# A sum of squared differences: other rows to other partitions, and the semaphores cleared by another engine

## The chip, the core and the metric

The kernel runs on one core of a Trainium2 chip. The metric is the device time of one execution in microseconds (us). The engines that matter are DVE (VectorE: subtracts), ACT (ScalarE: squares and sums), SP (SyncE: issues the transfers), POOL (GpSimd: sets four constants at the start) and the core's 16 DMA engines.

## The reference

```python
batch, dim = 1024, 4096
x, y: float32 of [batch, dim]
def reference(x, y, axis):        # axis = -1
    return np.sum((x - y) ** 2, axis=axis).astype(np.float32)
```

Two matrices of 16.8 MB each are read, and 1024 sums of 4 KB in all are written.

## The kernel before

**Layout.** There are 1024 rows for 128 partitions, so R = 8 rows lie together in one block of R x D = 32768 floats, 128 KiB, and each partition works on one block. The views `xv`, `yv` and `ov` (lines 60 to 62) say which: partition p takes block p. In SBUF the tensors X and Y hold six of the eight rows of a partition (`H = 6 * D`); the last two rows go into the places of the first two, when those are done with (`home`).

**Loads.** All 15 loads are issued by SP on one queue, each a column range of all 128 partitions (`load`, line 107). X comes in 6 ranges and Y in 9, with widths written out by hand: the first ones are 16384 and 16224 columns (64 KB and 63 KB per partition), then 8192, and then ever smaller ones down to 160 columns, so that little work is left after the last one. The first two are issued ahead of the program's opening barrier (`early`). The loads of the last two rows wait on L215 until ACT has squared the first and the second row.

**Work.** DVE waits for a range of Y and the X that goes with it, and subtracts in place, one row or part of a row at a time (`sub`, L170). ACT squares and sums each of these pieces (`square`, L176). Rows 6 and 7 come in several pieces; their partial sums lie in `parts` and are added by DVE (`complete`, L183). The last piece, of 160 columns, DVE squares and sums itself (L199).

**The end.** SP waits until the sums are there, issues the store of `results` (L227), and then calls `close` (lines 40 to 45):

```python
engine.sem_clear(range(self.sems[0].num, self.sems[-1].num + 1))
engine.wait_ge(stored, value).then_inc(stored, -value)
```

The first line sets the kernel's semaphores back to zero, as the next execution needs them. The semaphore `stored`, which the store counts up, isn't among them; the wait itself takes its 16 off again. There is no barrier at the end; the program is over when each engine has done its last instruction.

## Time and profile before

| | us |
|---|---|
| median of 3 runs (lowest to highest) | 84.36 (84.32 to 84.52) |
| the profiled execution | 84.36 |
| its span, from the first to the last instruction | 83.0 |
| DVE busy | 36.3 |
| ACT busy | 31.7 |
| POOL busy | 0.2 |
| DMA engines in use, as a share of 16 over the span | 95.2% |
| first subtraction on DVE | 40.89 |
| store issued on SP | 81.58 |

The span is shorter than the time, because the runtime opens and closes the program around it. A packet is what one DMA engine moves in one go; its record has a start, a duration and a size. "L170" is line 170 of the kernel.

### The profile page before, as it was taken

What the parts mean: (1) busy time and instruction counts of PE and PEld (TensorE: products, weight loads), DVE (VectorE), ACT (ScalarE), POOL (GpSimd) and SP (SyncE); (2) the same over time, 40 slices, a digit from 0 to 9 for tenths busy, and PEclk for the clock granted to TensorE, in tenths of its full rate; (3) what the DMA queues carried; (4) which work ended last, traced back from release to release, by engine and by line L of the source; (5) the groups of instructions that cost most, each with busy time, mean ns of one, the idle gap of its engine ahead of it and who ended that gap; (6) DMA issues with size and microseconds to landing.
All of it is one profiled execution on the core that took longest, in us unless ns stands there. A gap on an engine that the chain in (4) does not pass through costs nothing.

```text
span 83.0 us, 109 instructions
## 1 busy us (share of the span) xinstructions
DVE 36.3 (44%) x18; ACT 31.7 (38%) x27; POOL 0.2 (0%) x4
## 2 busy tenths in 40 slices
DVE  0000000000000000000299999999099995979981
ACT  0500000000000000000001969798970796989991
POOL 0000000000000000000000000000000000000000
DMA  9299999929999997599799979979999999999940
GB/s 505 95 410 505 505 505 505 505 95 410 500 500 500 500 500 313 219 469 500 332 426 505 474 316 474 505 332 426 424 429 429 400 435 439 426 407 404 395 145 2
DMA packets 2304, 33.56 MB, mean 404 GB/s; under 512 B 384, under 2 KB 768, under 8 KB 1408
## 3 DMA queue, kind: packets, MB, share of 16 engines
q1 hardware_dynamic: 2304, 33.56, 95.2%
HBM read 33.55 MB, written 0.00 MB: 404 GB/s over the span
## 4 chain that ended last, share of the span: by engine, by line
DMA 68%; ACT 14%; DVE 14%; SPq 1%; issue 0%
DMA Y<-in_y_dram 68%; ACT X L176 14%; DVE X L170 14%; SPq L107 1%; DVE results L183 0%; SPq L215 0%
## 5 line engine op out<-in xcount | busy, mean ns | idle before, releaser
L170 DVE TENSOR_TENSOR X<-X,Y 128x4096 f32<-128x4096 f32 (+9 forms) x14 | 35.8, 2593 | 44.9 <-DMA Y<-in_y_dram 44.8
L176 ACT ACTIVATE X<-X 128x4096 f32<-128x4096 f32 (+8 forms) x13 | 29.7, 2288 | 47.7 <-DVE X L170 47.7
L176 ACT ACTIVATION_READ_ACCUMULATOR X<-X 128x1 f32 x13 | 2.4, 188 | 0.0
L176 ACT ACT_TABLE_LOAD x1 | 1.3, 1283 | 1.9 <-PEq L19 1.9
L183 DVE TENSOR_REDUCE results<-parts 128x1 f32<-128x2 f32 (+1 forms) x2 | 0.3, 154 | 0.2 <-ACT X L176 0.2
L199 DVE CUSTOM_DVE_ANT_0 Y<-X,parts 128x160 f32<-128x160 f32 x1 | 0.4, 385 | 0.0
L245 POOL MEMSET const-bfloat16-1.0<- 128x1 bf16 x1 | 0.1, 102 | 0.0
L245 POOL MEMSET const-uint8-127<- 128x1 uint8 x1 | 0.1, 102 | 0.0
L245 POOL MEMSET const-float32-0.0<- 128x1 f32 x1 | 0.1, 99 | 0.2 <-issue 0.2
L245 POOL MEMSET const-float32-1.0<- 128x1 f32 x1 | 0.1, 99 | 0.0
L199 DVE DVE_READ_ACCUMULATOR2_ANT results<- 128x1 f32 x1 | 0.1, 83 | 0.0
## 6 DMA issues: line engine op xcount, KB each, us to landing
Y<-in_y_dram SPq DMA_DIRECT2D x1, 8112.0 KB, 40.4
X<-in_x_dram SPq DMA_DIRECT2D x1, 4096.0 KB, 48.7
Y<-in_y_dram SPq DMA_DIRECT2D x1, 4096.0 KB, 58.0
X<-in_x_dram SPq DMA_DIRECT2D x1, 2784.0 KB, 13.4
Y<-in_y_dram SPq DMA_DIRECT2D x1, 1456.0 KB, 19.2
Y<-in_y_dram SPq DMA_DIRECT2D x1, 1328.0 KB, 16.2
X<-in_x_dram SPq DMA_DIRECT2D x1, 912.0 KB, 21.0
Y<-in_y_dram SPq DMA_DIRECT2D x1, 464.0 KB, 21.6
```

The source lines that it names most:

```text
L107: nc.sync.dma_start(out=dst[:, home(c0, c1)], in_=src[:, c0:c1]).then_inc(sem, 16)
L170: nc.vector.tensor_sub(out=a, in0=a, in1=Y[:, home(c0, c1)]).then_inc(diffs, 1)
L176: nc.scalar.activation(out=a, in_=a, func=Square, accum_out=acc).then_inc(acts, 1)
L183: nc.vector.tensor_reduce(out=results[:, r : r + 1], in_=parts_of(r, len(row_parts[r])), axis=mybir.AxisListType.X, op=add,).then_inc(sums, 1)
L199: nc.vector.tensor_tensor_reduce(out=Y[:, home(*piece)], in0=X[:, home(*piece)], in1=X[:, home(*piece)], scale=1.0, scalar=parts_of(r, 1), ...
L245: nc = _bacc.Bacc("TRN2", target_bir_lowering=False, num_devices=1)
```

## The change

It has two parts, and some code is written in another way without another effect (`pieces_of` is written out where it was called, and `complete(6)` stands without its loop).

The first part is the layout. Partition p = 8e + i takes block 16i + e of the rows in place of block p, with e from 0 to 15 and i from 0 to 7. The source of a load is therefore an array of three dimensions, [16, 8, columns], whose first step is one block (128 KiB) and whose second is 16 blocks (2 MiB), while the destination stays [128, columns]. The store's destination is viewed in the same way.

The second part is the end. POOL waits for the store and then clears the semaphores, with `stored` now among them; SP's clear and SP's wait are gone.

```diff
-    def close(self, engine, stored, value):
-        engine.sem_clear(range(self.sems[0].num, self.sems[-1].num + 1))
-        engine.wait_ge(stored, value).then_inc(stored, -value)
+    def close(self, sem, value):
+        self.nc.gpsimd.wait_ge(sem, value)
+        self.nc.clear_and_free_semaphores(self.sems)
...
-    xv = x.rearrange("(p r) d -> p (r d)", p=P)
-    yv = y.rearrange("(p r) d -> p (r d)", p=P)
-    ov = out.rearrange("(p r) -> p r", p=P)
+    G = 8
+    xv = x.rearrange("(i e r) d -> e i (r d)", i=G, r=R)
+    yv = y.rearrange("(i e r) d -> e i (r d)", i=G, r=R)
+    ov = out.rearrange("(i e r) -> e i r", i=G, r=R)
...
-    stored = nc.alloc_semaphore("stored")
     diffs = prog.semaphore("diffs")
     acts = prog.semaphore("acts")
     sums = prog.semaphore("sums")
+    stored = prog.semaphore("stored")
...
-        nc.sync.dma_start(out=dst[:, home(c0, c1)], in_=src[:, c0:c1]).then_inc(sem, 16)
+        nc.sync.dma_start(out=dst[:, home(c0, c1)], in_=src[:, :, c0:c1]).then_inc(sem, 16)
...
     nc.sync.wait_ge(sums, n["sums"])
     nc.sync.dma_start(out=ov, in_=results).then_inc(stored, 16)
-    prog.close(nc.sync, stored, 16)
+    prog.close(stored, 16)
```

## The prediction

> **What bounds the kernel now.** I read the page first: its chain that ended last, then the DMA lines above it.

> ```profile
> span 83.0 us, 109 instructions
> ...
> DVE 36.3 (44%) x18; ACT 31.7 (38%) x27; POOL 0.2 (0%) x4
> ...
> DMA packets 2304, 33.56 MB, mean 404 GB/s; under 512 B 384, under 2 KB 768, under 8 KB 1408
> ...
> q1 hardware_dynamic: 2304, 33.56, 95.2%
> ...
> DMA 68%; ACT 14%; DVE 14%; SPq 1%; issue 0%
> ```

> The 16 DMA engines are in use for 95.2% of the span. 2304 packets are 16 transfers (15 loads, one store) of 128 rows plus 16 completion marks each, so a partition's row is one packet, up to 64 KB long. Is there slack in the streaming itself? The table by stretches answers that (columns: stretch, its length, busy time of DVE, ACT and POOL, clock, share of the DMA engines, GB/s):

> ```profile
> 20.00:30.00 10.00, 0.00 (x0) 0.00 (x0) 0.00 (x0) 1.00 0.96 415
> 30.00:40.00 10.00, 0.00 (x0) 0.00 (x0) 0.00 (x0) 1.00 0.96 415
> ```

> 415 GB/s at a share of 0.96 is 432 GB/s at a full share, 27 GB/s for each engine. The packet records say how even that is: of the first load's 128 packets of 65,536 B the later 112 take 2.418 to 2.420 us (27.1 GB/s), and the second load's 128 of 64,896 B take 2.394 to 2.399. There is no packet here that an address made slow. Only the first round differs: those 16 packets start between 1.01 and 1.64 us and take 2.68 to 3.43, on the mean 0.69 us above the later 2.42. Then the end, from the chain in order of time and the rows of SP's last lines:

> ```profile
> 53.87 16.23 DMA Y<-in_y_dram
> 70.09 0.02 issue
> 70.12 2.94 DVE X L170
> 73.05 0.02 issue
> 73.07 8.29 ACT X L176 x14
> 81.37 0.02 issue
> 81.39 0.16 DVE results L183
> ```
> ```profile
> 81.58 0.35 SPq L227 DMA_DIRECT2D out_dram<-results  x1
> ```
> ```profile
> L44 SPq EVENT_SEMAPHORE_RANGE_CLEAR  x1: 62/62/62, 82.0 to 82.0; - x1
> ```
> ```profile
> L45 SPq EVENT_SEMAPHORE  x1: 17/17/17, 83.0 to 83.0; - x1
> ```

> The loads are the pace until 70.09, ACT without a gap from 73.07 to 81.37, then the row sum, the store (issued 81.58, landed 1.4 us later by the page) and SP's wait for it at 83.01. The clear at 82.0 lies wholly inside the store's flight.

> **The time that the sum starts from.** The profiled execution took 84.36 us, which is the median of the three runs; 1.36 us of it lie around the span of 83.0. I sum against 84.36. Within 0.3% (0.25 us: 84.11 to 84.61) counts as the same, about what a measurement of this kernel can tell from no change.

> **Part one, the close.** Removed from SP: the clear (0.062, hidden) and the wait (0.017). Added on POOL: a wait for the store, behind which only POOL's clear is queued; POOL has had nothing to do since the memsets at 0.33, so nobody waits for it but the end of the program. The wait opens at the same landing, 83.0. What was hidden under the store is now behind it:
> - From the wait to the next instruction on POOL's queue: in the records of L19 POOL's waits start at 1.383 and 1.711 and the instruction behind each at 1.462 and 1.789, so 0.08 us.
> - The clear: 0.062 by SP's row. POOL's own rows bound it: 0.017 (its EVENT_SEMAPHORE) to 0.181 (its DRAIN on L245). One more such DRAIN in the library's call is possible. I take 0.062, the same operation, and one range, because the names are allotted in a row and "stored" now stands among them.
> - After the program the runtime lets the engines finish one after the other. The trace's semaphore records hold its marks (semaphore 2): a chain on the way up through the engines and back, nine marks with 0.023 to 0.111 us from one to the next. Now DVE's mark is there at 81.70, 0.15 after DVE's last instruction; SP's, the top of the chain, at 83.171, 0.14 after SP's wait; the next, going back, at 83.214. So from SP's end to the way back is 0.185. POOL's mark stands two places below SP's. When POOL is the last, the mark comes 0.14 after its end, and from it to the way back I take the same three hops of the undisturbed pass before the kernel: 0.045 + 0.023 + 0.111 = 0.18. That is 0.32 in place of 0.185, so 0.13 more. Bounds: 0 (if the marks don't wait in that order) to 0.13.

> Sum: 0.08 + 0.062 + 0.13 = 0.27. Bounds: 0.08 + 0.017 + 0 = 0.10 to 0.08 + 0.181 + 0.13 = 0.39. Not below nothing, since clear and wait stand behind the store in any case.

> **Part two, the rows' layout.** The bytes, the number of transfers, their sizes per partition (64 KB, 63 KB, 32 KB and on down) and all sums on DVE and ACT stay, so 36.3 and 31.7 us of engine time stay. Each load's source is now two nested steps, 16 of 128 KiB and within each 8 of 2 MiB, where it was 128 steps of 128 KiB.
> - Issue on SP: rows of L107 go from 0.33 to 0.43 us for an issue that doesn't meet a full queue, one form, so a different pattern is bounded by that spread, -0.1 to +0.1. Only the first load's issue (0.00 to 0.38) is on the path; the second overlaps the 21.7 us of the first, and the later ones stand behind tens of us of queued bytes. I take 0.02: one more counter.
> - The streaming: 77.4 us of the 79 us of data time is 2,097 KB per engine at 27.1 GB/s, at which the packets already run. The neighbouring blocks can't quicken what is even to 0.002 us a packet, so no gain from this is possible there by these rows. A loss is: see the rivals. Taken: 0.
> - The first round: 0.69 us over the later packets. It could be reading from 16 spread places at once, or mere first latency. The store bounds the latency: 1.4 us from issue to landing with hardly any data. The first load landed 21.7 us after issue; the second's 8112 KB took from 21.7 to 40.87, 19.1 us, which makes 19.3 for the first's 8192 KB. 21.7 - 19.3 = 2.4 us of start, of which the store's 1.4 is what any transfer shows; 1.0 is the most that a layout could win. Bounds -1.0 to +0.5 (the spread of the starts is 0.63). Taken: 0, because all 16 engines end the first round within 0.5 us of each other, however early they began, which reads as a common start and not as single places being slow.
> - The store: 128 packets of 32 B before and after, now to places 512 B apart for neighbouring partitions. Its packets take 7 to 9 ns; bounds -0.1 to +0.1, taken 0.

> If the first load lands later or earlier, DVE's first subtraction (40.89) moves with it, and so do L215's releases of the later loads, so the whole is shifted; ACT's run from 73.07 follows. What is late next is ACT: its 8.29 us can't shrink.

> Sum of all: 84.36 + 0.27 + 0.02 = 84.65. That is slower by 0.34%, hardly over the bound; the close's own bounds alone give 84.48 to 84.77.

> The trace can't say which partitions share one DMA engine, but it says that one engine moves 27 GB/s and all 16 together 432, so no two of them are now in each other's way. [...]

> **Rivals.**
> 1. [...] Mechanism: the first round's 0.69 us is 16 far places opened at once, and neighbouring blocks shorten it. For it: the excess is there in that round alone. Against: it ends in common. Price: -0.3 to -1.0 with the close at +0.29, so 83.65 to 84.35, middle 84.0. It decides when the start gives back more than 0.54 us (0.29 + 0.25), then it is faster.
> 2. *The loads lose a little.* Mechanism: another grouping of rows to engines makes the 16 finish less together, or a reading of 16 neighbours slows some packets. For it: ACT's last run hangs on a landing at 70.09, so each 1% of the 69 us before it costs 0.7 us. Against: nothing in the rows. 0.5 to 2% of the streaming is 0.35 to 1.4: 85.0 to 86.05.
> 3. *Pairs of engines share one way into the SBUF.* Mechanism: for a while of each load only half of the ways are in use. By rows: 432 GB/s for 16, 216 for 8. The data time of 79 us would double: 84.65 + 79 = 163; less where partners fall out of step. Against: nothing in the trace, which shows one grouping only.
> 4. *The change does nothing.* Layout neutral and the runtime's own closing hides POOL's clear: 84.4 to 84.6.

> **How the numbers follow.** Case of my sum (layout neutral, close +0.10 to +0.39, issue and store within 0.1): 0.45, of which a little over half lies above 84.61. Rival 4: 0.08. Rival 1: 0.18, most of it below 84.11. Rival 2: 0.14. Rival 3: 0.15. So slower 0.26 + 0.14 + 0.15 = 0.55, same 0.19 + 0.08 + 0.02 = 0.29, faster 0.16. The forecast is 84.65. The range runs from 83.9 (most of rival 1) to 86.05 (all of rival 2) and leaves out rival 3 and the far end of rival 1, under 0.2. The likeliest case by itself has 84.45 to 84.8.

> **What would show it.** Right: the span grows by about 0.15 us, the last rows are POOL's wait at 83.0 and its clear of about 0.06 close behind, the time outside the span grows by about 0.13; the first load lands 21.7 us after issue, 415 GB/s at 0.96 between 20 and 40. Rival 1: the first load lands in 21.4 or less and every later landing is earlier by as much. Rival 2: landings drift apart, GB/s between 20 and 40 falls below 412. Rival 3: about half the GB/s at a full share, packets of 64 KB at 4.8 us. I am wrong altogether if the packets leave 2.42 us in either direction, or if POOL's clear takes much over 0.2.

## The result, and the profile after

The changed kernel takes 164.93 us (median of four, 163.76 to 166.37) beside 84.42 for the kernel before: the ratio is 1.949, with a 95% interval of 1.938 to 1.960; it leaves out the slowest of the four runs, which took over 1.5% longer than the fastest. The forecast was 84.65 with a range of 83.9 to 86.05. What came has the signs of rival 3, which had 0.15 and stood outside the range.

The page of the changed kernel, the same lines that were shown of before; the profiled execution took 163.76 us:

```profile
span 161.9 us, 109 instructions
...
DVE 36.4 (23%) x18; ACT 32.2 (20%) x27; POOL 0.2 (0%) x4
...
DMA packets 2304, 33.56 MB, mean 207 GB/s; under 512 B 384, under 2 KB 768, under 8 KB 1408
...
q1 hardware_dynamic: 2304, 33.56, 97.2%
```

The bytes, the 2304 packets and the engines' work are what they were. The DMA engines are in use for 97.2% of a span twice as long, so they aren't waiting for issues or for room in SBUF: each packet takes twice as long. In the packet records 16 are in flight at 10, 25, 35 and 100 us, so all 16 engines work; eight at work would not explain the 5 us either, since eight packets of that size by themselves, to every 12th partition in a probe below, took 2.45 to 3.21. The table by stretches (columns as before):

```profile
20.00:30.00 10.00, 0.00 (x0) 0.00 (x0) 0.00 (x0) 1.00 1.00 210
30.00:40.00 10.00, 0.00 (x0) 0.00 (x0) 0.00 (x0) 1.00 1.02 210
```

That is 210 GB/s at a full share in place of 415 at 0.96 (a packet counts where it starts, so a share can come out a little under or over 1). In the packet records the first load's rows of 65,536 B have a median of 5.10 us, where they took 2.42. From its issues, with the KB and the us to landing:

```profile
Y<-in_y_dram SPq DMA_DIRECT2D x1, 8112.0 KB, 82.3
...
X<-in_x_dram SPq DMA_DIRECT2D x1, 43.1
out_dram<-results SPq DMA_DIRECT2D x1, 4.0 KB, 1.8
```

The first load of X lands after 43.1 us (21.7 before), the second load after 82.3 (40.4), the store after 1.8 (1.4). From the chain in order of time:

```profile
96.21 45.74 DMA Y<-in_y_dram
...
141.97 2.92 DVE X L167
...
156.90 0.81 another core or an unknown queue
...
157.73 0.70 DVE X L167
...
158.46 1.16 ACT X L173 x4
...
159.64 0.16 DVE results L180
```

ACT's run without a gap at the end, 8.29 us before, is gone; it now waits for pieces of the last rows, and the loads set the pace to the last one: their last packet ends at 158.14, and "another core or an unknown queue" is a wait whose releaser the profile can't name. POOL's end stands where the prediction put it, behind the store:

```profile
L46 POOLq DRAIN  x1: 88/88/88, 161.7 to 161.7; - x1
L46 POOLq EVENT_SEMAPHORE_RANGE_CLEAR  x1: 138/138/138, 161.8 to 161.8; - x1
```

### The profile page after: what moved, and what is told of

Its sections match the earlier page's. It is cut to its first block, busy times and chain, and to the rows that moved or that the text cites. A ratio compares the mean times of both kernels' runs of the same rounds, so it can differ in the third digit from the quotient of the medians.

```text
span 161.9 us, 109 instructions
## 1 busy us (share of the span) xinstructions
DVE 36.4 (23%) x18; ACT 32.2 (20%) x27; POOL 0.2 (0%) x4
## 2 busy tenths in 40 slices
DMA packets 2304, 33.56 MB, mean 207 GB/s; under 512 B 384, under 2 KB 768, under 8 KB 1408
## 3 DMA queue, kind: packets, MB, share of 16 engines
q1 hardware_dynamic: 2304, 33.56, 97.2%
## 4 chain that ended last, share of the span: by engine, by line
DMA 55%; another core or an unknown queue 29%; DVE 11%; ACT 3%; SPq 0%; issue 0%; DVEq 0%
DMA Y<-in_y_dram 28%; DMA X<-in_x_dram 27%; DVE X L167 11%; ACT X L173 3%; SPq L110 0%; DVE results L180 0%; DVEq L163 0%; SPq L217 0%
## 6 DMA issues: line engine op xcount, KB each, us to landing
Y<-in_y_dram SPq DMA_DIRECT2D x1, 8112.0 KB, 82.3
```

## The experiments

Three theories of the doubled packets. The outer count is the number of steps in the first dimension of a load's source, 16 in the change and 128 before; a way into the SBUF is theory A's word for an entrance through which DMA engines write to some of the partitions, and no record shows one. **A**: with an outer count of 16, one DMA engine gets eight partitions in a row, and then two engines at a time write through one way into the SBUF. **B**: the HBM gives neighbouring blocks only half the rate. **C**: a source of two nested steps is slow by itself.

### The two parts, each alone

The new end alone (`e1_close`: the kernel before with the diff's `close`, and `stored` among the names):

> Only the new end: partition p takes block p as before, but POOL waits for the store and clears the semaphores behind it. All theories of the doubled loads agree that the streaming stays at its 2.42 us per packet of 65,536 B, so the time tells what the end alone costs. My prediction's term: +0.27 us, 84.65. From the changed kernel's own trace (POOL's last instruction ends 0.28 us after the store's last landing, and the runtime's closing mark of POOL comes 0.53 us after that, where SP's came 0.14 after): +0.7 to +0.8, 85.1.

Measured: 85.31 us beside 84.44, 1.0103 times before (1.0086 to 1.0121), +0.87. The streaming is untouched (415 GB/s at 0.96 between 20 and 40 us).

The new layout alone (`e2_layout`: the diff's four lines for `xv`, `yv`, `ov` and `src[:, :, c0:c1]`, with the end of the kernel before):

> Only the new layout: partition 8e + i takes block 16i + e, and the end is that of the kernel before. Theory A (an engine now has eight partitions in a row, and engines n and n + 4 write through one way into the SBUF), theory B (the HBM gives 16 neighbouring blocks only half the rate) and theory C (a source of two nested steps is slow by itself) all expect nearly the whole loss here: 163.5 to 165 us, packets of 65,536 B at about 5.1 us. If the end were at fault in any large part, it would be near 85.

Measured: 165.2 us, 1.954 (1.946 to 1.962). The layout is the whole of the loss; the end's 0.87 is lost among the differences between executions at that pace.

### The same idea with another outer count

```diff
-    G = 8
+    G = 4
```

on top of the layout alone (`e3_g4`).

> The same edit with 4 in place of 8: partition 4e + i takes block 32i + e, so the source still has two nested steps (32 of 128 KiB, 4 of 4 MiB) and neighbouring partitions' groups still read neighbouring blocks, but the outer step now counts 32, four partitions each; the end is that of the kernel before. Theory A: a group of four partitions can be dealt to engines as in the plain transfer, one way into the SBUF each, so packets stay at 2.42 us and the time at 84.4 plus the longer issue of the first load (0.65 in place of 0.38 us, so 84.6 to 84.9). Theory B (neighbouring blocks) and theory C (two nested steps): 150 us and over, packets near 5 us.

Measured: 85.37 us beside 84.44, 1.0112 (1.0094 to 1.0130). The table by stretches and two of its issues:

```profile
20.00:30.00 10.00, 0.00 (x0) 0.00 (x0) 0.00 (x0) 1.00 0.96 415
```
```profile
X<-in_x_dram SPq DMA_DIRECT2D x1, 22.4
out_dram<-results SPq DMA_DIRECT2D x1, 4.0 KB, 1.8
```

Two nested steps, and groups of partitions that read neighbouring blocks, at the old rate. Theory C falls. B is weakened and not refuted, because no record shows which blocks are read at one time. The 0.93 that it loses is over the 0.2 to 0.5 that was expected, which had priced the first load alone. Two nested steps show at the two places where nothing hides them: the first load lands after 22.4 us in place of 21.7 (21.8 to 22.0 in three other runs with the plain source), the store after 1.8 in place of 1.4. In SP's rows for the loads the shortest issue went from 0.42 us (Y) and 0.33 (X) to

```profile
L108 SPq DMA_DIRECT2D Y<-in_y_dram x9: 593/603/4870, 0.7 to 65.5; - x9
L108 SPq DMA_DIRECT2D X<-in_x_dram x6: 534/603/1310, 0.0 to 59.2; - x6
```

### The same shape with far addresses

```diff
-    xv = x.rearrange("(i e r) d -> e i (r d)", i=G, r=R)
+    rows = [[7 * N, P // G], [N, G], [1, N]]
+    xv = bass.AP(x.tensor, x.offset, rows)
```

and so for `yv`, with the plain `ov` (`e6_near`).

> The new layout's shape with nearly the old addresses: partition 8e + i reads block 7e + i, so the source has two nested steps, 16 of 7 blocks and 8 of one, the groups of eight partitions read 896 KiB apart, and no 16 neighbouring blocks are read at once; the end is that of the kernel before. Some blocks are read twice and others not at all, so the sums belong to other rows than the reference's. Theory A (the outer count of 16 deals eight partitions in a row to one engine; engines share ways into the SBUF): 163 to 166 us, packets of 65,536 B near 5.1 us. Theory B (16 neighbouring blocks halve the HBM's rate): 85.0 to 85.6 us, packets near 2.42 us, as with partition 4e + i.

Measured: 165.35 us, 1.955 (1.946 to 1.964), 210 GB/s between 20 and 40 us. The outer count of 16 is enough: the far blocks of the new layout took 165.2 us, these near ones 165.35. Its store, with one step, lands in 1.4 us again.

### The plain layout, half of the partitions at a time

```diff
-        nc.sync.dma_start(out=dst[:, home(c0, c1)], in_=src[:, c0:c1]).then_inc(sem, 16)
+        for h in (0, 64):
+            nc.sync.dma_start(
+                out=dst[h : h + 64, home(c0, c1)], in_=src[h : h + 64, c0:c1]
+            ).then_inc(sem, 16)
```

with DVE's waits for the loads at 32 (`e5_halves`).

> The kernel before, its plain rows and one-step sources, but each load is issued as two, partitions 0 to 63 and then 64 to 127. All 16 engines then write to one half of the partitions at a time. Theory A (32 partitions apart share one way into the SBUF, so each half of the partitions has eight ways): nearly the loss of the change without its layout, 160 to 170 us, packets of 65,536 B near 5 us. Theory B (neighbouring blocks of the HBM) and theory C (a source of two nested steps): 84.4 to 87 us, packets near 2.42, with some cost of 15 more issues.

Measured: 164.94 us, 1.949 (1.932 to 1.966), packets of 65,536 B with a median of 5.12 us. No row of HBM is read from elsewhere and no source has two steps; there are 15 more transfers, and other partitions are written at one time. The issues aren't the limit: the DMA engines are in use for 97.7% of the span. That is theory A's loss without the change.

### The ways by themselves

In four probes SP issues one transfer after the other, each behind the landing of the one before. One row of 64 KB per engine goes to chosen partitions; the records don't name a packet's engine, but the rows run side by side (eight packets of 7.4 to 8.6 us in a wait of 10.6 us). Each probe ran once. The first (`e4_ports`) has, for example, `out=A1[0:8]`, `A1[0:32:4]`, `A1[0:64:8]`, `A1[0:128:16]`, all from `xv[0:8]`.

> A probe in place of the computation: no sums, zeros are stored. Transfers of 64 KB rows are issued one after the other, each behind the one before; the first four read the same eight blocks of x, one row per DMA engine, and differ only in the partitions written: 0 to 7 in a row; every 4th from 0 to 28; every 8th from 0 to 56; every 16th from 0 to 112. Then 16 rows to every 5th partition from 0 to 75, and the same 16 to every 8th from 0 to 120. Theory A, with one way into the SBUF for the four partitions 4m to 4m + 3 and those 32 above: packets of 0 to 7 four times as long (9.7 us), every 4th 2.42, every 8th and every 16th twice as long (4.8), every 5th both kinds in one transfer (10 rows long, 6 near 2.4, as counted from that map), every 8th of 16 rows 4.8. Theories B and C: all of the first four alike, near 2.4 to 3.4 us, since source and shape are the same.

SP's waits (waiting line, who is waited for, total us, times, longest); the wait at a line is for the transfer issued before it, so L71 is for partitions 0 to 7, L74 for every 4th, L77 for every 8th, L80 for every 16th, and L83 and L86 are for 16 rows to every 5th and to every 8th:

```profile
SPq L71 <- DMA A<-in_x_dram: 10.6, 1, 10.6
SPq L86 <- DMA A<-in_x_dram: 6.8, 1, 6.8
SPq L83 <- DMA A<-in_x_dram: 6.7, 1, 6.7
SPq L80 <- DMA A<-in_x_dram: 6.6, 1, 6.6
SPq L77 <- DMA A<-in_x_dram: 6.4, 1, 6.4
SPq L74 <- DMA A<-in_x_dram: 4.3, 1, 4.3
```

The same eight rows of x, in the same shape, wait 4.3 us or 10.6 us by where they go. By packet: 2.42 to 3.06 us to every 4th partition, 4.07 to 4.91 to every 8th, 3.95 to 4.59 to every 16th, 7.4 to 8.6 to eight in a row. By theory A's map, as the expectation has it, that is one, two, two and four engines to a way; four take less than four times as long as one, and no run here shows why. The 16 rows to every 8th partition were slow as forecast (4.29 to 5.35). The miss is the 16 rows to every 5th: six were to be quick, and all took 4.09 to 5.07.

The second probe (`e7_ports2`) asks whether an engine is slow at another's partitions even alone:

> A second probe in place of the computation (no sums, zeros are stored): 64 KB rows, one per engine, one transfer at a time. In order: 8 rows to every 5th partition (0 to 35), blocks 0 to 7; 8 rows to every 12th (0 to 84), blocks 0 to 7; 10 rows to every 12th (0 to 108), blocks 0 to 9; 16 rows to every 7th (0 to 105), blocks 0 to 15; the same partitions, every 8th block; 16 rows to every 5th (0 to 75), every 4th block; 16 rows to every 8th (0 to 120), every 8th block. Theory A with single ways (32 partitions apart share one): first 6 rows at 2.4 to 3.1 us and 2 near 4.5; second and third all at 2.4 to 3.1; fourth and fifth 12 rows at 2.4 to 3.1 and 4 near 4.5; sixth 6 and 10; seventh all near 4.5. Theory A2 (an engine that writes to another way than the one which it serves in the plain transfer is slow by itself, sharing or not): all of them near 4.5. Theory B for the 16-row transfers (neighbouring blocks): fourth slow, fifth to seventh at 2.4 to 3.1.

```profile
SPq L88 <- DMA A<-in_x_dram: 7.1, 1, 7.1
SPq L85 <- DMA A<-in_x_dram: 6.9, 1, 6.9
SPq L79 <- DMA A<-in_x_dram: 6.7, 1, 6.7
SPq L82 <- DMA A<-in_x_dram: 6.5, 1, 6.5
SPq L70 <- DMA A<-in_x_dram: 6.4, 1, 6.4
SPq L73 <- DMA A<-in_x_dram: 4.4, 1, 4.4
SPq L76 <- DMA A<-in_x_dram: 4.3, 1, 4.3
```

The first three (L70, L73, L76) are theory A's numbers: of 8 rows to every 5th partition six packets took 2.76 to 3.26 us and two 4.49 and 4.62, and these are partitions 0 and 35, if the map holds; the 8 and the 10 rows to every 12th all took 2.45 to 3.21. So theory A2 falls. The four transfers of 16 rows (L79 to L88) were all slow in every row, with neighbouring blocks and with every 8th, which A's simple form doesn't give.

The third (`e10_ports3`) looks for the count at which the quick rows vanish:

> A third probe in place of the computation (no sums, zeros are stored): 64 KB rows, one per engine, to every 7th partition, in transfers of 8, 10, 12, 14, 15 and 16 rows, one after the other. By the map of theory A one pair shares a way with 8 rows (partitions 0 and 35), and two pairs from 10 rows on (28 and 63 too), so the pure map expects 6 of 8, 6 of 10, 8 of 12, 10 of 14, 11 of 15 and 12 of 16 rows at 2.4 to 3.3 us. In the probe before, all 16 of 16 were slow. If the number of engines at work does that (something that they share further up), the quick rows vanish at some count between 10 and 16; if the second pair does it, they vanish at 10.

With 8 rows six took 2.45 to 3.32 us and two 4.28 and 4.48. With 10, 12, 14, 15 and 16 rows every one took 3.64 to 5.06. They vanish at 10, where by the map the second pair comes in. The fourth (`e11_ports4`) parts the second pair from the number of engines:

> A fourth probe in place of the computation (no sums, zeros are stored): 64 KB rows, one per engine. In order: 15 rows to every 9th partition (0 to 126), by the map of theory A 15 different ways into the SBUF and no pair, blocks 0 to 14; 9 rows to every 7th (one pair, 0 and 35); 8 rows to every 3rd (two pairs, 0 and 3, 12 and 15, and four rows by themselves); 10 rows to every 6th (two pairs and six by themselves); the first once more with every 8th block. If sharing a way is all that counts for a transfer's slowness: the first and the last all quick, at 2.4 to 3.5 us, however many engines; the second 7 quick and 2 near 4.5. If a second pair slows the rows that share nothing: the third and fourth have no quick row. If instead engines 8 and up at a partition below 64 do that: the second and the fourth have none, and the third has 4 quick rows. If the number of engines did it: the first and the last all near 4.5.

```profile
SPq L76 <- DMA A<-in_x_dram: 6.4, 1, 6.4
SPq L79 <- DMA A<-in_x_dram: 6.2, 1, 6.2
SPq L73 <- DMA A<-in_x_dram: 6.0, 1, 6.0
SPq L82 <- DMA A<-in_x_dram: 4.8, 1, 4.8
SPq L70 <- DMA A<-in_x_dram: 4.5, 1, 4.5
```

L70 and L82 are for the 15 rows on 15 different ways by the map: all at 2.47 to 3.30 us, from blocks 0 to 14 and from every 8th. So 15 engines read 15 neighbouring blocks without loss, which is the end of theory B. With one pair (L73) seven packets took 2.47 to 3.21 and two 4.00 and 4.41. With two pairs (L76, 8 rows; L79, 10 rows) all took 3.69 to 4.83, the unshared ones too.

### What the new end costs, and why

The clear behind the store, but on SP (`e8_sp_behind`: the two lines of `close` in the other order):

> The kernel before with SP's two last instructions in the other order: SP waits for the store and clears the semaphores behind it, so the clear is no longer hidden, but POOL has no part in it. If the price of the new end is that the clear stands behind the store: 85.1 to 85.3 us. If it is that POOL is the engine that does it: 84.44 + 0.06 for the clear + up to 0.08 between the two instructions, 84.5 to 84.6.

Measured: 84.62 us beside 84.53, 1.0010 (0.9997 to 1.0023): no difference that counts. Only the wait on POOL, with the clear left on SP under the store (`e9_pool_wait`):

```diff
-        engine.wait_ge(stored, value).then_inc(stored, -value)
+        self.nc.gpsimd.wait_ge(stored, value).then_inc(stored, -value)
```

> The kernel before with the wait for the store moved to POOL and the clear left on SP under the store's flight. In the run with the new end alone, POOL's last instruction ended 0.28 us after the last landing, and the runtime's mark of POOL came 0.53 us after that. If that mark is late whenever POOL is the last to finish: 84.44 + 0.4 to 0.6, 84.85 to 85.05. If it is late because of the clear on POOL: 84.44 + about 0.13 for the two more hops, 84.55 to 84.65.

Measured: 85.09 us beside 84.53, 1.0067 (1.0046 to 1.0087), +0.56. So by the medians over half of the end's 0.87 is that POOL is the last to finish, even with a wait alone. The trace's semaphore records show where: SP's closing mark comes 0.13 to 0.14 us after SP's last instruction (`e8_sp_behind` and before), POOL's 0.53 (`e1_close`) and 0.56 (`e9_pool_wait`) after POOL's.

## Why the prediction was wrong

**The step that failed** is "The streaming", with the value 0 taken. The step read the packets of before, even to 0.004 us (the later 112 of the first load have 2.418 to 2.422), and concluded rightly that nothing was there to gain. For the loss it took the same evenness as a reason for 0. It is none: by theory A's map the probes' packets are quick where no two engines share a way (15 rows on 15 ways, 2.47 to 3.30 us) and slow where they do (eight rows in four pairs, 3.95 to 4.91 us), and by theory A the change makes all of them share. The trace of before shows one grouping of partitions to engines and can't price another. In place of the 0 the runs showed 5.10 us a packet for 2.42, and the layout alone took 165.2 us for 84.44.

**Rival 3 had nearly the price, and the mechanism as far as the probes show it.** It gave 163 from the doubled data time (84.65 + 79 is 163.65); 164.93 came. Its packets were forecast at 4.8 us and took 5.1. In the packet records the loads' data time, as a mean over the 16 engines, went from 78.9 us to 157.0, which is 1.99 times. The rows of 22,272 B and over went from 65.3 to 133.5 us, 2.05 times, and the shorter ones from 13.6 to 23.5, 1.73 times. So the price came that near partly by luck: it was too low for the long rows and too high for the short ones. Its argument against, "nothing in the trace, which shows one grouping only", was an absence of evidence, written down as if it weighed. The probes bear the mechanism out in part: in the three transfers whose only pair on one way, by theory A's map, is partitions 0 and 35, two rows were slow (4.00 to 4.62 us), and 15 rows on 15 ways of that map are all quick (2.47 to 3.30); that two pairs and more slow every row (3.64 to 5.06 us) the map doesn't give. That an outer count of 16 gives one engine eight partitions in a row, and that the engines then meet in pairs, is the author's inference and not shown, since the records don't name a packet's engine. What the runs show is the time by outer count: with two nested steps 16 takes 165.2 and 165.35 us with far and with near blocks, and 32 takes 85.37.

**Partners don't fall out of step in the long rows.** "Less where partners fall out of step" allowed for a smaller loss. There it didn't come: the packets of the first load's later rounds took 4.88 to 5.13 us. The short rows near the end lose less: packets of 2048 B took 0.111 us in the median, 0.084 before, and those of 640 B 0.032 in both. Whether that is partners out of step, no run here shows.

**The close** was sized at 0.27 and cost 0.87. In the records of the new end alone the way from the store's last landing to the closing chain's way back grew by 0.75 us, from 0.22 to 0.97. The hops back were right (0.12 for 0.13). POOL's own two instructions cost 0.25 more than SP's wait, not 0.14, because the library's call is a DRAIN of 0.088 and a clear of 0.138, where SP's 0.062 was taken; the DRAIN was named as possible and left out of the sum. The rest, 0.39, was a term set at no difference: that POOL's mark follows its end as soon as SP's does. The 0.1 between this 0.75 and the 0.87 needs no cause: the interval of the ratio is 0.73 to 1.02 us.

**The issue of two nested steps** was sized at 0.02 on the strength of the spread of one form's rows, and cost about 0.9 in all in the run with the outer count of 32. Its trace shows the first packet at 1.41 us for 1.01, of which 0.26 is the longer first issue (0.64 for 0.38), and the store at 1.8 for 1.4 us, which the prediction had taken at 0. The "rows of one form" could not bound another form.

**Rival 1** is refuted by the fourth probe: its 15 rows were as quick from neighbouring blocks as from every 8th (2.47 to 3.30 us for both). In the run with the outer count of 32 the 16 packets of the first round took 3.04 us on the mean, 3.10 before (an excess of 0.68 over 2.42, not 0.69) and 3.08 to 3.19 in three other runs with the plain source; which blocks they read at one time is not shown. There was nothing to win. The "common start" reading of the first round fits, since in that run the later start moved the ends with it (4.59 to 5.17 us for 3.98 to 4.47).

What stays open: why a second shared way slows the rows that share nothing, and why the doubled packets take 5.1 us and not 4.84. The probes show both and explain neither.

## What to carry to other kernels

Keep the count of 128 as the outermost dimension of a load's source (84.44 us here; 32 took 85.37 and 16 took 165.2), and look at the packets' duration, not at the number of engines in use: the share was 97.2% at half the rate. When a change alters which rows go to which engine, the even packets of the kernel before are no evidence; price the new grouping by a probe of one row per engine before anything else. Let the last instruction of a program stand on SP and not on POOL (a wait on POOL in place of SP cost 0.56 us here). What must be cleared can go under the store, though behind it on SP it cost nothing that stands clear of noise (84.62 us for 84.53).
